# A two-layer mixing trunk on one core: rows by transposes of spread columns, weights cast ahead of the modulated input, two of u's weights split inside the first step

## The chip, the core and the metric

The kernel runs on one core of a Trainium2 chip. The core has five engines with a queue each: TensorE (PE, matmuls; PEld is its weight load), VectorE (DVE), ScalarE (ACT), GpSimd (POOL) and SyncE (SP), which here only issues DMAs. The metric is the device time of one execution in microseconds (us). The kernel before takes 1035.68 us, the median of three runs (1033.89 to 1036.2).

## What is computed

Two layers over x (512 tokens by 1024 features) and a conditioning row c of 1024:

```
mod = silu(c) @ ada_w[l] + ada_b[l]           # 6 rows of 1024: shift, scale, gate, twice
h   = x * (1 + scale1) + shift1
a, u, v = split(h @ w_in[l])                  # 512 features each
y_a = pool_mixer(a)                           # trailing means over 2, 4, 8, 16 tokens, a 128x128 product, a scale
y_b = gelu(u) * (tril(W_s) @ norm(gelu(v)) + b)
x   = layernorm(2**0.5 * x + gate1 * ([y_a, y_b] @ w_out[l]))
h   = x * (1 + scale2) + shift2
g, val = split(h @ w_up[l])                   # 2816 features each
x   = layernorm(2**0.5 * x + gate2 * ((gelu(conv3(g)) * val) @ w_down[l]))
```

## The kernel before

**Products in three parts.** Every large product of a weight w and an activation h is made of three matmuls on rounded float32 (float32r): w_hi h_hi, w_hi h_lo and w_lo h_hi. A weight arrives as a tile `raw` of 128x1024 (512 KB) by DMA. ACT casts it to `whi` (L158), DVE subtracts to get `wlo` (L161). `refill` does this for the next weight of a fixed list `order`; `get` hands the oldest split weight out. There are four `raw` tiles and six pairs `whi`, `wlo`; a weight split "in units" takes tiles of 128x512 from the pool of 29 `unit` tiles instead. The engines run their queues in the order in which the code is written; nothing is reordered by a scheduler.

**The modulation row by row sums.** `mod` is not made on PE. A tile of `ada_w` (128 outputs by 1024 inputs, 512 KB) is multiplied on DVE by the row `c2` (2 silu(c), the same on all partitions) and summed along the row (`ada_sum`, L208): one sum gives 128 values, as one column of `modc`. There are 96 sums. 16 of them (shift and scale of the first norm) belong to the first step below. The others are put between other work by `pump(n)`; 24 of those (gate 1, scale 2, shift 2 of layer 0) must be done before the first norm's result is modulated. The text calls them sum 1 to sum 24. Sums read from seven tiles: three `ada` and, until x is loaded into them, four `xr`. `ada_load` fills tiles that are free, and waits on SP for the sum that read the tile before.

**Rows on all partitions.** `c2` is made by 16 matmuls of spread columns of c (hi and lo) against an identity, into two banks, and two copies on ACT (L97 to L109). Eighteen matmuls `idle` follow. A gate must be a row on all partitions too: `gate_start` makes, on DVE, four 128x512 tiles of identity times columns (L229 to L235), and `ada_flush`, two calls later, sums them on PE by a product with ones (L256, L257), two copies on ACT (L258).

**The first step.** The a and v parts of layer 0's input projection run over the eight 128-feature slices k of h. For each k: two sums, the columns A0 and B0 (L500, L503), then on ACT h_hi (L504) and h in full (L505), then on DVE h_lo (L508). `FIRST[k]` lists the weights that come in at step k: 0 to 3 are a's, 8 to 11 are v's (4 to 7 are u's and come after). In a step the code writes: h of k+1, h_lo of k, the casts and subtractions of the weights for k+1, and then the matmuls of k.

**After it** come, in layer 0, the copies of a (L592), pooling on DVE (`pool_group`), the norm of v on ACT, the four tiles of u (`u_tile`, 24 matmuls each), the pool products (`pool_mix`, L615), the gating products (`z_mms`), then the out projection: its first half is `project` (L369 to L371, tile out), its second `project_and_norm` (tile n_pj), in which the first norm waits for the gate and for all 24 sums. `MIX_FILL` and `OUT_FILL` say how many sums are pumped at each place. The gated MLP follows, and layer 1.

Of the kernel before, what the change touches and what calls it, by code (L numbers as in the profile page):

```python
# [26 lines left out]
FIRST = ((8, 0), (1,), (9, 2), (3,), (10,), (), (11,), ())  # L27
N_UNITS, N_RAW, N_ADA, N_SPLIT = 29, 4, 3, 6
AHEAD, N_IDLE = 2, 18
X_AT = 14  # L30
MIX_FILL, OUT_FILL = (3, 3, 3, 2, 1, 1), (2, 3, 3, 3)
# [8 lines left out]
def trunk(ctx: ExitStack, tc: tile.TileContext, a: dict, out: bass.AP):  # L40
# [52 lines left out]
    c_hl = [const.tile([P, KD], F32R, name=f"c_{n}") for n in ("hi", "lo")]  # L93
    V.tensor_copy(c_hl[0], c_th)
    V.tensor_tensor(c_hl[1], c_th, c_hl[0].bitcast(F32), op=ALU.subtract)
    c2 = const.tile([P, D], F32, name="c2")
    for hf in range(2):  # L97
        ps = bank(f"c2_{hf}")
        for j in range(4):
            k = 4 * hf + j  # L100
            for i, part in enumerate(c_hl):
                T.matmul(
                    ps[:, j * P : (j + 1) * P],
                    part[:, k : k + 1].to_broadcast([P, P]),
                    ident_r,
                    start=i == 0,
                    stop=i == 1,
                )
        A.copy(c2[:, halves(hf)], ps)  # L109

    idle = bank("idle")
    for i in range(N_IDLE):
        T.matmul(idle[:, :P], ident_r, ident_r, start=True, stop=True)
    ones_r = const.tile([P, P], F32R, name="ones_r")
    V.tensor_copy(ones_r, ones)
# [8 lines left out]
    for l in range(L):  # L124
        w_in = (0, 1, 2, 3, 8, 9, 10, 11) if l else [i for f in FIRST for i in f]
        order += [("w_in", (l, i)) for i in (*w_in, 4, 5, 6, 7)]
        order += [("w_out", (l, hf, i)) for hf in range(2) for i in range(4)]
        for j0, j1 in STAGES:
            order += [("w_up", (l, j, gv)) for j in range(j0, j1) for gv in range(2)]
            order += [("w_down", (l, hf, i)) for hf in range(2) for i in range(j0 // 2, j1 // 2)]  # L130
# [93 lines left out]
    def gate_start(l, v):  # L224

        g = modc[l][:, 8 * v : 8 * v + 8]
        gh = small.tile([P, KD], F32R, tag="gh", name=f"gh{l}_{v}")
        gl = small.tile([P, KD], F32R, tag="gl", name=f"gl{l}_{v}")
        V.tensor_copy(gh, g)  # L229
        V.tensor_tensor(gl, g, gh.bitcast(F32), op=ALU.subtract)  # L230
        out_ = []
        for hf in range(2):
            for part in (gh, gl):
                d = unit(f"gd{l}_{v}_{hf}", F32R)
                V.tensor_tensor(  # L235
                    d.rearrange("p (j n) -> p j n", j=4),
                    ident.unsqueeze(1).to_broadcast([P, 4, P]),
                    part[:, 4 * hf : 4 * hf + 4].bitcast(F32).unsqueeze(2).to_broadcast([P, 4, P]),
                    op=ALU.mult,
                )  # L240
                out_.append(d)
        return out_

    def ada_flush(now=False):


        for due in ada_due:
            due[0] += 1
            if due[3] is None and (now or due[0] >= 2):
                due[3] = gate_start(*due[1:3])  # L250
        while ada_due and (now or ada_due[0][0] >= 4):
            _, l, v, d = ada_due.pop(0)
            gates[l, v] = rows.tile([P, D], F32, tag="gate", name=f"gate{l}_{v}")
            for hf in range(2):
                ps = bank(f"gate{l}_{v}_{hf}")
                T.matmul(ps, ones_r, d[2 * hf], start=True, stop=False)  # L256
                T.matmul(ps, ones_r, d[2 * hf + 1], start=False, stop=True)  # L257
                A.copy(gates[l, v][:, halves(hf)], ps)  # L258

    def pump(n=1, upto=None):  # L260

        for _ in range(n):
            i = ada_at["step"]
            if i >= len(ada) or (upto is not None and ada[i][:2] not in upto):
                return
            ada_load(len(ada_free))
            l, v, n_ = ada[i]
            ada_sum(l, v, n_, ada_raw.pop(0))
            if n_ == KD - 1:
                o = slice(8 * v, 8 * v + 8)  # L270
                V.tensor_tensor(modc[l][:, o], modc[l][:, o], cols[l][:, C_ADAB + 8 * v : C_ADAB + 8 * v + 8], op=ALU.add)
                if v in (2, 5):
                    ada_due.append([0, l, v, None])
            ada_at["step"] += 1
# [210 lines left out]
    def first_load(k):  # L485

        if k >= KD:
            ada_load(len(ada_free))
            return
# [78 lines left out]
    for l in range(L):  # L568
# [156 lines left out]
        else:  # L725
            refill(1)
# [175 lines left out]
```

## Time and profile before

| | us |
|---|---|
| median of three runs | 1035.68 |
| the profiled execution | 1035.5 |
| its span, first to last instruction | 1033.8 |
| PE busy in it | 992.7 (96%) |
| DVE busy | 661.8 (64%) |
| ACT busy | 363.5 (35%) |
| POOL busy | 104.1 (10%) |

The profiled execution is 1.7 us longer than its span, and 0.2 us under the median. Times within it are counted from the span's start. The first 200 us are the part in which PE is not always busy: PE is at 9 tenths or more in 35 of the page's 40 slices, and four of the five others lie before 200 us. A wait is put down to what ended it; a row of a timeline gives start, length, engine, line, operation, and in brackets the idle time before it with what ended that.

### The profile page before, as it was taken

Reading aid. Unit: us, or ns where it says so; the run is one execution under the profiler, and the core shown is the slowest. Engines: PE = TensorE matmul, PEld = TensorE weight load, DVE = VectorE, ACT = ScalarE, POOL = GpSimd, SP = SyncE. Lnnn points to the kernel's source line nnn. Section 1 sums busy time; section 2 is a strip of 40 time slices with the busy share of each in tenths; the row PEclk is TensorE's granted clock in tenths of the full one; section 3 lists DMA queues with packets and bytes.
Section 4 is the critical chain, followed back from the end, with each engine's and each line's share of the span. In section 5 each row is a group of like instructions: output and inputs, shape, how many; then the busy total and the mean of one; then the engine's idle time right before and its main releaser. Section 6 shows DMA issues by size and latency. Waiting matters only on the chain.

```text
span 1033.8 us, 11992 instructions
## 1 busy us (share of the span) xinstructions
PE 992.7 (96%) x4676; PEld 828.6 (80%) x4676; DVE 661.8 (64%) x931; ACT 363.5 (35%) x531; POOL 104.1 (10%) x80
## 2 busy tenths in 40 slices
PE   7999868999999999999999999999999999999996
PEld 5777657888888888888889878898888888888886
DVE  5769877887771466747589763978554245544456
ACT  4362317433431123334155440743343222333210
POOL 0020003600000000000038100360000000000002
PEclk9999979999999999999999999999999999999999
DMA  9876553375563335546413321326332333223302
GB/s 354 322 246 207 207 207 122 107 281 205 204 223 102 101 130 188 193 154 253 163 61 116 129 73 62 102 102 229 118 102 82 102 101 98 90 98 102 123 1 81
DMA packets 46232, 153.54 MB, mean 149 GB/s; under 512 B 7264, under 2 KB 7520, under 8 KB 46176
## 3 DMA queue, kind: packets, MB, share of 16 engines
q1 hardware_dynamic: 46176, 152.78, 42.3%
q8 instruction: 36, 0.59, 0.2%
q14 instruction: 20, 0.16, 0.1%
HBM read 150.67 MB, written 2.10 MB: 148 GB/s over the span
## 4 chain that ended last, share of the span: by engine, by line
PE 82%; DVE 10%; DMA 2%; ACT 2%; issue 2%; POOL 1%; SPq 0%; DVEq 0%; POOLq 0%
PE up L197 15%; PE up L198 15%; PE up L196 15%; PE down L370 6%; PE down L371 6%; PE down L369 6%; DVE wlo L161 2%; PE u L198 1%; DVE xr L208 1%; DMA ada<-in_ada_w_dram 1%; PE u L196 1%; PE u L197 1%; PE n_pj L371 1%; PE n_pj L370 1%; PE n_pj L369 1%
## 5 line engine op out<-in xcount | busy, mean ns | idle before, releaser
L197 PE MATMUL up<-hl,whi 128*128 128x512 f32 (+1 forms) x768 | 286.1, 372 | 2.3 <-DVE hl L346 2.3
L198 PE MATMUL up<-hh,wlo 128*128 128x512 f32 (+1 forms) x768 | 286.0, 372 | 1.4 <-DVE wlo L161 1.4
L196 PE MATMUL up<-hh,whi 128*128 128x512 f32 (+1 forms) x768 | 286.3, 373 | 0.0
L161 DVE TENSOR_TENSOR wlo<-raw_w_up,whi 128x1024 fp32r<-128x1024 f32 x88 | 118.6, 1353 | 138.2 <-ACT whi L158 138.2
L197 PEld LDWEIGHTS up<-hl,whi 128*128 128x128 f32 x768 | 145.4, 189 | 27.5 <-DVE hl L346 2.7
L198 PEld LDWEIGHTS up<-hh,wlo 128*128 128x128 f32 x768 | 145.4, 189 | 26.6 <-DVE wlo L161 1.8
L196 PEld LDWEIGHTS up<-hh,whi 128*128 128x128 f32 x768 | 145.5, 189 | 25.1
L161 DVE TENSOR_TENSOR wlo<-raw_w_down,whi 128x1024 fp32r<-128x1024 f32 x44 | 53.9, 1225 | 114.0 <-ACT whi L158 114.0
L158 ACT CAST whi<-raw_w_up 128x1024 fp32r<-128x1024 f32 x88 | 90.9, 1045 | 57.0 <-PE down L371 52.6
L369 PE MATMUL down<-whi,gh 128*128 128x512 f32 x272 | 105.8, 389 | 0.0
L370 PE MATMUL down<-wlo,gh 128*128 128x512 f32 x272 | 105.8, 389 | 0.0
L371 PE MATMUL down<-whi,gl 128*128 128x512 f32 x272 | 105.8, 389 | 0.0
L208 DVE SCALAR_TENSOR_TENSOR ada<-ada,c 128x1024 f32<-128x1024 f32 x80 | 97.0, 1217 | 8.6 <-DMA ada<-in_ada_w_dram 4.5
L796 ACT ACTIVATE y<-y 128x512 f32<-128x512 f32 x44 | 27.9, 633 | 152.0 <-DVE y L793 152.0
L158 ACT CAST whi<-raw_w_down 128x1024 fp32r<-128x1024 f32 x44 | 46.0, 1047 | 74.3 <-PE down L371 74.3
L786 ACT ACTIVATE y<-up,cols 128x512 f32<-128x512 f32 x44 | 34.3, 779 | 80.5 <-PE up L198 80.5
L343 ACT ACTIVATE ht_n<-tr_n,B,A 128x128 f32<-128x128 f32 x96 | 36.0, 455 | 67.3 <-PE tr_n L331 67.3
L369 PEld LDWEIGHTS down<-whi,gh 128*128 128x128 f32 x272 | 51.1, 188 | 10.7
L370 PEld LDWEIGHTS down<-wlo,gh 128*128 128x128 f32 x272 | 51.1, 188 | 10.6
L371 PEld LDWEIGHTS down<-whi,gl 128*128 128x128 f32 x272 | 51.1, 188 | 10.5
L304 POOL TENSOR_SCALAR rs_n<-mv_n 128x1 f32<-128x1 f32 x12 | 7.2, 601 | 497.6 <-DVE mv_n L302 497.6
L161 DVE TENSOR_TENSOR wlo<-raw_w_in,whi 128x1024 fp32r<-128x1024 f32 x24 | 37.6, 1587 | 22.3 <-ACT whi L158 22.3
(169 smaller groups left out, 1469.4 us busy)
## 6 DMA issues: line engine op xcount, KB each, us to landing
raw_w_up<-in_w_up_dram SPq DMA_DIRECT2D x88, 512.0 KB, 3.7
ada<-in_ada_w_dram SPq DMA_DIRECT2D x80, 512.0 KB, 3.8
raw_w_down<-in_w_down_dram SPq DMA_DIRECT2D x44, 512.0 KB, 3.7
raw_w_in<-in_w_in_dram SPq DMA_DIRECT2D x24, 512.0 KB, 5.8
xr<-in_ada_w_dram SPq DMA_DIRECT2D x16, 512.0 KB, 7.0
raw_w_out<-in_w_out_dram SPq DMA_DIRECT2D x16, 512.0 KB, 4.5
xT<-in_xT_dram SPq DMA_DIRECT2D x8, 256.0 KB, 8.9
xr<-in_x_dram SPq DMA_DIRECT2D x4, 512.0 KB, 4.9
```

The costliest lines, as they stand in the source:

```text
L158: A.copy(hi, src)
L161: (eng or V).tensor_tensor(lo, src, hi.bitcast(F32), op=ALU.subtract)
L196: T.matmul(ps, w[0], x[0], start=start, stop=False)
L197: T.matmul(ps, w[0], x[1], start=False, stop=False)
L198: T.matmul(ps, w[1], x[0], start=False, stop=stop)
L208: V.scalar_tensor_tensor(raw, raw, 0.5, c2, op0=ALU.mult, op1=ALU.mult, accum_out=modc[l][:, o : o + 1])
L343: A.activation(tmp[:, w], ps[hf][:, w], AF.Identity, bias=cb[:, k : k + 1], scale=ca[:, k : k + 1])
L369: T.matmul(ps[:, f], ah[:, cs], wh, start=i + j == 0, stop=False)
L370: T.matmul(ps[:, f], ah[:, cs], wl, start=False, stop=False)
L371: T.matmul(ps[:, f], al[:, cs], wh, start=False, stop=i + j == n - 1)
L786: A.activation(y, pg, AF.Identity, bias=col[:, C_CB + j : C_CB + j + 1], scale=col[:, cw + 2 : cw + 3])
L796: A.activation(y, y, AF.Gelu_apprx_tanh)
```

## The change

- `c2` and the gates are made by one function, `spread`: a column of 128 values, read as if it stood 128 times side by side, is transposed on PE against the float32 identity, which gives the row on all partitions; eight transposes and two copies for 1024 values. The hi and lo columns of c, `gate_start`, its tiles and `ones_r` go. Five idle matmuls stand before c2's transposes and twenty behind them; c2's second half is copied by DVE.
- In the first step the casts of the weights for k+1 are written ahead of h of k+1, and their subtractions behind A0 and B0 and ahead of h_lo of k+1. h_lo of k+1 is written in step k, before k's matmuls.
- Weights 4 and 5 (u's first two) come in at steps 5 and 7 of the first step, split in units.
- A gate is transposed at the second `ada_flush` after its last sum, not the fourth.
- `pump` loads one tile fewer than are free. In the last two steps of the first step `first_load` loads two and three tiles.
- `MIX_FILL` is (6, 3, 2, 2, 1, 1) for (3, 3, 3, 2, 1, 1), `OUT_FILL` (2, 2, 3, 2) for (2, 3, 3, 3).

```diff
-FIRST = ((8, 0), (1,), (9, 2), (3,), (10,), (), (11,), ())
+FIRST = ((8, 0), (1,), (9, 2), (3,), (10,), (4,), (11,), (5,))
-AHEAD, N_IDLE = 2, 18
+AHEAD, N_IDLE = 2, (5, 20)
-MIX_FILL, OUT_FILL = (3, 3, 3, 2, 1, 1), (2, 3, 3, 3)
+MIX_FILL, OUT_FILL = (6, 3, 2, 2, 1, 1), (2, 2, 3, 2)
...
+    def spread(to, col, second=A.copy):
+        for hf in range(2):
+            ps = bank("spread")
+            for j in range(4):
+                k = 4 * hf + j
+                T.transpose(ps[:, j * P : (j + 1) * P], col[:, k : k + 1].to_broadcast([P, P]), ident)
+            (second if hf else A.copy)(to[:, halves(hf)], ps)
...
+    idle_mms(N_IDLE[0])
+    spread(c2, c_th, V.tensor_copy)
+    idle_mms(N_IDLE[1])
...
     def ada_flush(now=False):
         for due in ada_due:
             due[0] += 1
-            if due[3] is None and (now or due[0] >= 2):
-                due[3] = gate_start(*due[1:3])
-        while ada_due and (now or ada_due[0][0] >= 4):
-            _, l, v, d = ada_due.pop(0)
+        while ada_due and (now or ada_due[0][0] >= 2):
+            _, l, v = ada_due.pop(0)
             gates[l, v] = rows.tile([P, D], F32, tag="gate", name=f"gate{l}_{v}")
-            for hf in range(2):
-                ps = bank(f"gate{l}_{v}_{hf}")
-                T.matmul(ps, ones_r, d[2 * hf], start=True, stop=False)
-                T.matmul(ps, ones_r, d[2 * hf + 1], start=False, stop=True)
-                A.copy(gates[l, v][:, halves(hf)], ps)
+            spread(gates[l, v], modc[l][:, 8 * v : 8 * v + 8])
...
-            ada_load(len(ada_free))
+            ada_load(len(ada_free) - 1)
...
         if k >= KD:
-            ada_load(len(ada_free))
+            ada_load(k - KD + 2)
             return
...
+    def first_w(k, defer=None):
+        for i in FIRST[k]:
+            refill(1, None, defer, in_units=3 < i < 8)
...
-    refill(len(FIRST[0]), None, late)
+    refill(1, None, late)
     first_h(0, *firsts[0])
-    for f in late:
-        f()
+    late.pop()()
+    refill(1, None, late)
+    first_lo(0)
+    late.pop()()
...
         if k + 1 < KD:
+            first_w(k + 1, late)
             first_h(k + 1, *firsts[k + 1])
-        first_lo(k)
-        refill(len(FIRST[k + 1]) if k + 1 < KD else 1)
+            for f in late:
+                f()
+            late.clear()
+            first_lo(k + 1)
...
+    ready[:0] = u_w
...
         else:
-            refill(1)
             pump(MIX_FILL[0], fill)
```

**ACT, the first step's beginning.** Before (whi are casts of weights, hh is h_hi, the write to xT is h in full; whi_177, 180 and 207 are weights 8, 0 and 1):

```order
L158 CAST whi_177<-raw_w_in_167 128x1024
L158 CAST whi_180<-raw_w_in_169 128x1024
L504 ACTIVATE hh<-xT_165,B_0_158,A_0_157 128x512
L505 ACTIVATE xT_165<-xT_165,B_0_158,A_0_157 128x512
L504 ACTIVATE hh<-xT_173,B_0_158,A_0_157 128x512
L505 ACTIVATE xT_173<-xT_173,B_0_158,A_0_157 128x512
L158 CAST whi_207<-raw_w_in_175 128x1024
```

Now (whi_170, 180, 194 are the same weights):

```order
L156 CAST whi_170<-raw_w_in_160 128x1024
L475 ACTIVATE hh<-xT_158,B_0_151,A_0_150 128x512
L476 ACTIVATE xT_158<-xT_158,B_0_151,A_0_150 128x512
L156 CAST whi_180<-raw_w_in_162 128x1024
L156 CAST whi_194<-raw_w_in_168 128x1024
L475 ACTIVATE hh<-xT_166,B_0_151,A_0_150 128x512
L476 ACTIVATE xT_166<-xT_166,B_0_151,A_0_150 128x512
```

The cast of weight 0 has gone behind h of k = 0, and the cast of weight 1 ahead of h of k = 1.

**DVE, from the last h_lo of the first step to the pooling** (ada and xr with modc are the sums, wlo the weights' low parts, ws the pooling). Before:

```order
L508 TENSOR_TENSOR hl<-xT_365,hh 128x512
L508 TENSOR_TENSOR hl<-xT_402,hh 128x512
L161 TENSOR_TENSOR wlo_481<-raw_w_in_478,whi_480 128x1024
L611 TENSOR_SCALAR psc_532<-cols_87 128x1 x4
L161 TENSOR_TENSOR wlo_540<-raw_w_in_508,whi_539 128x1024
L208 SCALAR_TENSOR_TENSOR ada_80,modc_153<-ada_80,c_106 128x1024
L208 SCALAR_TENSOR_TENSOR xr_81,modc_153<-xr_81,c_106 128x1024
L208 SCALAR_TENSOR_TENSOR xr_82,modc_153<-xr_82,c_106 128x1024
L602 TENSOR_TENSOR ws_0_550<-at_524 128x511
```

Now:

```order
L479 TENSOR_TENSOR hl<-xT_406,hh 128x512
L593 TENSOR_SCALAR psc_537<-cols_87 128x1 x4
L206 SCALAR_TENSOR_TENSOR ada_80,modc_146<-ada_80,c_102 128x1024
L206 SCALAR_TENSOR_TENSOR xr_81,modc_146<-xr_81,c_102 128x1024
L206 SCALAR_TENSOR_TENSOR xr_82,modc_146<-xr_82,c_102 128x1024
L206 SCALAR_TENSOR_TENSOR xr_83,modc_146<-xr_83,c_102 128x1024
L206 SCALAR_TENSOR_TENSOR xr_84,modc_146<-xr_84,c_102 128x1024
L206 SCALAR_TENSOR_TENSOR ada_78,modc_146<-ada_78,c_102 128x1024
L584 TENSOR_TENSOR ws_0_556<-at_529 128x511
```

The low parts of weights 4 and 5 (wlo_481, wlo_540) have gone from here into the first step, and three more sums stand ahead of the pooling.

**DVE, in the out projection, from the last low part of mix (ml) on.** Before:

```order
L667 TENSOR_TENSOR ml_856<-z_852,mh_855 128x512
L161 TENSOR_TENSOR wlo_896<-raw_w_out_840,whi_895 128x1024
L208 SCALAR_TENSOR_TENSOR ada_79,modc_153<-ada_79,c_106 128x1024
L208 SCALAR_TENSOR_TENSOR ada_80,modc_153<-ada_80,c_106 128x1024
L229 CAST gh_2_929<-modc_153 128x8
L230 TENSOR_TENSOR gl_2_930<-modc_153,gh_2_929 128x8
L235 TENSOR_TENSOR gd_2_0_933<-ident,gh_2_929 128x512
L235 TENSOR_TENSOR gd_2_0_935<-ident,gl_2_930 128x512
L235 TENSOR_TENSOR gd_2_1_937<-ident,gh_2_929 128x512
L235 TENSOR_TENSOR gd_2_1_939<-ident,gl_2_930 128x512
L161 TENSOR_TENSOR wlo_942<-raw_w_out_862,whi_941 128x1024
L208 SCALAR_TENSOR_TENSOR ada_78,modc_153<-ada_78,c_106 128x1024
```

Now:

```order
L649 TENSOR_TENSOR ml_872<-z_868,mh_871 128x512
L159 TENSOR_TENSOR wlo_913<-raw_w_out_856,whi_912 128x1024
L206 SCALAR_TENSOR_TENSOR ada_78,modc_146<-ada_78,c_102 128x1024
L242 TENSOR_TENSOR modc_146<-modc_146,cols_87 128x8
L206 SCALAR_TENSOR_TENSOR ada_79,modc_146<-ada_79,c_102 128x1024
L159 TENSOR_TENSOR wlo_948<-raw_w_out_878,whi_947 128x1024
L206 SCALAR_TENSOR_TENSOR ada_80,modc_146<-ada_80,c_102 128x1024
L206 SCALAR_TENSOR_TENSOR ada_78,modc_146<-ada_78,c_102 128x1024
```

The six instructions of the gate are gone; the sums that follow are numbers 16 on, where before they were 14 on. (The row with modc and cols adds the bias.)

## Rows read from the trace of the kernel before

**Rows 1.** Busy us: PE, PEld, DVE, ACT, POOL (instructions); granted clock, DMA share, GB/s

```profile
62.45:122.67 60.22, 55.68 (x240) 43.20 (x239) 53.84 (x98) 25.73 (x46) 6.71 (x9) 0.97 0.60 202
...
122.67:147.76 25.09, 14.02 (x49) 10.20 (x47) 19.34 (x36) 1.64 (x2) 0.79 (x2) 0.80 0.74 271
...
200.00:1033.80 833.80, 820.92 (x3861) 688.13 (x3859) 510.32 (x677) 281.92 (x399) 68.59 (x49) 1.00 0.38 131
```

**Rows 2.** Waits of PE from 0 to 200 us: total, times, longest

```profile
PE n_pj L370 <- DVE wlo L161: 7.5, 2, 5.1
```

**Rows 3.** Timeline, PE, the first turn: start, length, engine, line, operation [idle <- releaser]

```profile
147.76 1.09 PE L331 MATMUL tr_n<-ident,xr 128*128 128x128 f32 x8 [3.59 <-DVE xr L416]
```

**Rows 4.** Timeline, DVE and ACT, one k of the first step

```profile
33.39 1.22 DVE L208 SCALAR_TENSOR_TENSOR ada<-ada,c 128x1024 f32<-128x1024 f32 x1
...
35.87 0.68 DVE L508 TENSOR_TENSOR hl<-xT,hh 128x512 fp32r<-128x512 f32 x1
...
35.99 0.82 ACT L504 ACTIVATE hh<-xT,B,A 128x512 fp32r<-128x512 f32 x1 [3.78 <-DVE B L503]
...
38.63 1.23 DVE L161 TENSOR_TENSOR wlo<-raw_w_in,whi 128x1024 fp32r<-128x1024 f32 x1 [2.08 <-ACT whi L158]
...
39.77 1.22 DVE L208 SCALAR_TENSOR_TENSOR xr<-xr,c 128x1024 f32<-128x1024 f32 x1
```

**Rows 5.** Timeline, ACT and PE, where the first step begins

```profile
9.62 1.04 ACT L158 CAST whi<-raw_w_in 128x1024 fp32r<-128x1024 f32 x1 [2.18 <-DMA raw_w_in<-in_w_in_dram]
...
10.89 1.04 ACT L158 CAST whi<-raw_w_in 128x1024 fp32r<-128x1024 f32 x1 [0.23 <-DMA raw_w_in<-in_w_in_dram]
...
13.30 0.75 PE L546 MATMUL a<-hh,wlo 128*128 128x512 f32 x1
...
16.90 1.09 PE L549 MATMUL v<-whi,hl 128*128 128x512 f32 x4
```

**Rows 6.** Busy us by stretch, 10 to 20 us

```profile
10.00:20.00 10.00, 7.05 (x23) 4.87 (x23) 7.23 (x12) 5.80 (x7) 0.00 (x0) 1.00 1.03 411
```

**Rows 7.** Timeline, PE, the first products of u's tiles and the pool products

```profile
62.45 0.39 PE L196 MATMUL u<-hh,whi 128*128 128x512 f32 x1
...
67.89 1.02 PE L645 MATMUL rw<-wst,ones 128*128 128x512 f32 x2
...
74.20 0.39 PE L196 MATMUL u<-hh,whi 128*128 128x512 f32 x1
...
84.08 1.88 PE L615 MATMUL pm<-ws,poolw 128*128 128x512 f32 x4
...
91.29 1.02 PE L615 MATMUL pm<-ws,poolw 128*128 128x512 f32 x2
```

**Rows 8.** Timeline, ACT and DVE, between the first step and u's third tile

```profile
61.06 2.06 ACT L592 COPY at<-a 128x512 f32<-128x512 f32 x4 [1.12 <-PE a L549]
...
68.67 0.69 DVE L602 TENSOR_TENSOR ws<-at 128x511 f32<-128x511 f32 x1
...
72.50 1.04 ACT L158 CAST whi<-raw_w_in 128x1024 fp32r<-128x1024 f32 x1
...
76.08 1.22 DVE L161 TENSOR_TENSOR wlo<-raw_w_in,whi 128x1024 fp32r<-128x1024 f32 x1
```

**Rows 9.** Timeline, SP, issues of the small constants

```profile
53.45 0.67 SPq L578 DMA_DIRECT2D poolw<-in_pool_w_dram  x1
...
62.79 0.58 SPq L66 DMA_DIRECT2D raw_w_in<-in_w_in_dram  x1
```

**Rows 10.** Loads into the tiles ada, 0 to 145 us

```profile
DMA to landing us min/median/max: 3.2/5.2/9.6
```

**Rows 11.** Timeline, DVE, end of the out projection to the first norm

```profile
116.08 1.22 DVE L161 TENSOR_TENSOR wlo<-raw_w_out,whi 128x1024 fp32r<-128x1024 f32 x1
...
123.32 1.22 DVE L208 SCALAR_TENSOR_TENSOR ada<-ada,c 128x1024 f32<-128x1024 f32 x1
...
141.72 0.68 DVE L321 TENSOR_TENSOR res<-out,gate 128x512 f32<-128x512 f32 x1
```

More of the change, by code (lines that the diff above doesn't have):

```diff
@@ L92, in trunk, with idle_mms @@
     V.scalar_tensor_tensor(c_th, c_th, 1.0, c_in, op0=ALU.add, op1=ALU.mult)
-    c_hl = [const.tile([P, KD], F32R, name=f"c_{n}") for n in ("hi", "lo")]
-    V.tensor_copy(c_hl[0], c_th)
-    V.tensor_tensor(c_hl[1], c_th, c_hl[0].bitcast(F32), op=ALU.subtract)
     c2 = const.tile([P, D], F32, name="c2")
-    for hf in range(2):
[L98 to L109, printed above, removed]
-    idle = bank("idle")
[L112 to L115, printed above, removed]
+    def spread(to, col, second=A.copy):
[5 more added lines that the diff above has]
+            (second if hf else A.copy)(to[:, halves(hf)], ps)
+    idle = bank("idle")
+    def idle_mms(n):
+        for i in range(n):
+            T.matmul(idle[:, :P], ident_r, ident_r, start=True, stop=True)
+    idle_mms(N_IDLE[0])
+    spread(c2, c_th, V.tensor_copy)
+    idle_mms(N_IDLE[1])
     neg_half = const.tile([P, 1], F32, name="neg_half")
@@ L125, in trunk @@
         w_in = (0, 1, 2, 3, 8, 9, 10, 11) if l else [i for f in FIRST for i in f]
-        order += [("w_in", (l, i)) for i in (*w_in, 4, 5, 6, 7)]
+        order += [("w_in", (l, i)) for i in (*w_in, *(i for i in range(4, 8) if i not in w_in))]
         order += [("w_out", (l, hf, i)) for hf in range(2) for i in range(4)]
@@ L222, in ada_load @@
                 ada_at["load"] += 1
[L224 to L242, printed above, removed]
     def ada_flush(now=False):
@@ L272, in pump @@
                 if v in (2, 5):
-                    ada_due.append([0, l, v, None])
+                    ada_due.append([0, l, v])
             ada_at["step"] += 1
@@ L508, in first_lo @@
         V.tensor_tensor(hl[:, k, :], firsts[k][0], hh[:, k, :].bitcast(F32), op=ALU.subtract)
+    def first_w(k, defer=None):
+        for i in FIRST[k]:
+            refill(1, None, defer, in_units=3 < i < 8)
     v_ps = [bank(f"v0_{c}") for c in range(NCH)]
-    a_ps, a_w, v_w, firsts, late = [], [], [], [], []
+    a_ps, a_w, v_w, u_w, firsts, late = [], [], [], [], [], []
     for k in range(2):
         first_load(k)
-    refill(len(FIRST[0]), None, late)
+    refill(1, None, late)
     first_h(0, *firsts[0])
-    for f in late:
-        f()
+    late.pop()()
+    refill(1, None, late)
+    first_lo(0)
+    late.pop()()
     for k in range(KD):
@@ L521, in trunk @@
         for i in FIRST[k]:
-            w = get()
-            if i < 8:
+            if i >= 8:
+                v_w.append(get())
+            elif i < 4:
                 a_ps.append(bank(f"a0_{i}"))
-                a_w.append(w)
+                a_w.append(get())
             else:
-                v_w.append(w)
+                u_w.append(get())
         if k + 1 < KD:
+            first_w(k + 1, late)
             first_h(k + 1, *firsts[k + 1])
-        first_lo(k)
-        refill(len(FIRST[k + 1]) if k + 1 < KD else 1)
+            for f in late:
+                f()
+            late.clear()
+            first_lo(k + 1)
         for ps, w in zip(a_ps[old:], a_w[old:]):
```

1 line of the change is left out of this document (removed).

## The prediction

> **What bounds the kernel now.** I read the busy time by stretch first, then PE's waits, then the timelines of DVE, ACT and PE where PE waits.
>
> From 200 us on PE is busy 820.92 of 833.80 us at a granted clock of 1.00, and DVE 510 [rows 1]. Work that is taken from DVE or ACT there frees nobody. Before it, from 62.45 to 147.76 us, DVE is busy 73.2 of 85.3 us, and from 122.67 on PE works only 14.02 of 25.09 us, at a mean granted clock of 0.80, between its levels of 1.2 and 2.4 GHz [rows 1]. PE's largest wait there is for low parts of weights, 7.5 us [rows 2], which stand on DVE behind sums. The first norm's result is turned at 147.76, after a wait of 3.59 us for DVE [rows 3]. So DVE's order sets the end of the first norm, and what follows hangs on that. I cut the way to 147.76 into four stretches, and the sum is the shift of that row.
>
> **First step, up to u (62.45 us).** In one k DVE does two sums and the columns (33.39 to 35.87, 2.48 us), h_lo (0.68), then waits 2.08 us for a cast that ACT does only after h, and makes one low part (38.63 to 39.77, 1.14): a period of 6.38 us [rows 4]. With the cast ahead of h, the low part starts at once. h takes ACT two passes of about 0.82 [rows 4], so h_lo is free some 1.75 us after the columns, 0.6 after the low part. The period becomes 2.48 + 1.14 + 0.6 + 0.65 = 4.9 us.
>
> The beginning pays for it. Weight 8 is cast at 9.62, when it lands; weight 0 lands at 10.89 [rows 5]. Now h of k = 0 comes between them: 10.66 to about 12.35 on ACT, then weight 0 until 13.4, its low part until 14.65. PE's second product needs that; before, it ran at 13.30 [rows 5]. From there to the end of k = 0 (16.90 and four products of 0.227, 17.81) it is 4.5 us, part of it at half pace [rows 5]: end at 19.15. Weight 1 lands 1.83 MB after weight 0; at 411 GB/s [rows 6] that is 4.5 us, 15.4, so its cast ends at 16.4, and k = 1 finds all it needs. 24 products take 67.89 - 62.45 = 5.44 us [rows 7], 0.2267 each. k = 1 to 7 have 21, 27, 33 and four times 24, 177 in all, 40.1 us: u begins at 59.3 instead of 62.45, if nothing is late. The one close place is the low part of weight 2, ready about 24.35 by the chain above, wanted at 24.4. From k = 3 on DVE is ahead: h of k = 7 is ready at about 18 + 6 x 4.9 + 1.1 = 48.5, wanted at 53.9. That slack of 5 us also covers weights 4 and 5, whose casts now ride in ACT's and DVE's free time.
>
> Gain 3.15 us. Bounds: +3.8 if the first products lose nothing to the new order; -1.7 if PE stays at half pace through k = 1 as well (21 x 0.23 = 4.8 us more). I take 3.15, since rows 5 shows the pace to come back within the first 15 products.
>
> c2 by eight transposes instead of sixteen matmuls I cost at nothing either way: h of k = 0 waits for ACT's cast at 9.62 [rows 5]. If that cover went, the price would be the sums' own time, two of 1.2 us [rows 4].
>
> **u and the pool products, to 91.29 us.** Before, u's first tile takes 5.44, ones times W_s and the second tile 6.31 (67.89 to 74.20), the third 9.88 (to 84.08), the first two pool products and the fourth tile 7.21 [rows 7]. The third is 4.44 over 5.44: it waits for the low part at 76.08, which stands behind five DVE pieces that began at 68.67 (two poolings and three sums, 7.41 us) [rows 8], and then runs at half pace for a while. Now three more sums stand ahead of the poolings, six in all. Five have their tiles loaded within the first step, and run from about 50 us, when DVE has nothing else; the load of the sixth is issued behind u's other weights and the small constants, a block of 9.3 us before [rows 9], which can begin when weight 5 lands (15.4 + 5.7 + 5 x 4.5 = 43.5); 5.2 us for its landing [rows 10] make 58. So poolings and three sums end at 59.2 + 7.4 = 66.6. The cast for that third tile came 11.44 us after the copies of a [rows 8], with the cast of weight 5 (1.04) in it. It starts at 57.9 + 10.4 = 68.3; low part by 70.6. The tile starts at 59.3 + 5.44 + 6.31 = 71.05 and wants the low part 0.45 later. The wait goes, by a margin of 0.9 us.
>
> Added on PE: gate 1's transposes behind the third tile, eight, 1.09 us as the eight at 147.76 [rows 3]. So the second pair of pool products comes at 59.3 + 5.44 + 6.31 + 5.44 + 1.09 + 7.21 = 84.8, instead of 91.29: gain 6.5 us so far.
>
> **Mixing to the out projection, 91.29 to 116.08.** From the pool products each step waits for the one before (PE, ACT's high part, cast, DVE's low part, gating, cast), with as many sums between as before. I carry its 24.79 us [rows 7, 11] over: 109.6.
>
> **The last sums, 116.08 to 147.76.** Before, 116.08 to 123.32 (7.24 us) holds a low part, sums 14 and 15, the gate's pieces and another low part [rows 11]. Sums 14 and 15 are now in the mixing, where DVE waits for casts anyway; the gate's pieces are gone; the second low part moves in among the later sums. 1.14 us is left, so sum 16 starts at 110.7, 12.6 us earlier. From there to the first norm's residual it is 18.40 us before [rows 11]. Nine sums, two low parts and the columns are 9 x 1.2 + 2 x 1.14 + 0.6 = 13.7 us; the other 4.7 are waits for loads, since only three tiles are left for the sums (the `xr` tiles hold x by then). A tile is filled when its sum is done, and the load takes 5.2 us in the median [rows 10]. The third low part (1.14) falls into these waits, so I keep 18.40, then 6.04 to the turn [rows 3, 11]: 135.1 instead of 147.76. PE is not later than that: the second block of products starts after the last low part, and there were 3.59 us to spare.
>
> Here the Trainium skill has another price. Its page DMA: Bandwidth & Descriptors (Anatomy of one DMA) puts a transfer at about 2.0 us fixed and bytes over 436 GB/s; for 512 KB that makes 3.2 us, an estimate by that page. The 26 loads here took 3.2 at least and 5.2 in the median [rows 10], so the trace agrees only with its best case. By the page the waits would vanish, which is the first rival below.
>
> **The rest.** Three more gates are made after 200 us: four matmuls become eight transposes, at most 0.2 us of PE each [rows 3]; DVE's pieces were hidden. `pump` now leaves one tile empty, which puts each load behind the next weight on SP; with a sum every few us after 200 that is hidden too. Eight more `unit` tiles are held until u's second tile is done; from 71 us on they are free. I cost all of this at nothing, bounds +-0.6.
>
> **Sum.** 147.76 - 135.1 = 12.6 us. The profiled execution took 1035.5 us, 1.7 beyond its span: 1022.9. It lies 0.2 under the median of the runs, so I say 1023.
>
> **Rivals.**
> 1. The last sums find their tiles loaded. The shallower queue of loads (half of 411 GB/s is unused before 122 us [rows 1, 6]) may land them nearer the 3.2 of rows 10. Then sum 16 to the residual is work alone, with the third low part 14.8 instead of 18.4: 3.6 us more gain, 1019.3. Against it: the same weights share the queue in that stretch, at 271 GB/s on the mean [rows 1].
> 2. The loads come a step later. A tile left empty costs up to one sum, 1.2 us, in each of the two rounds of three tiles: 2.4 us, 1025.4. For it: PE waits there for what stands on DVE behind such sums [rows 2].
> 3. The sixth sum blocks DVE. If the block of small constants starts no earlier than before, at 53.45 [rows 9], the load lands at 68, the low part of u's third tile comes at 77.8 instead of being wanted at 71.5, and 6.3 us are lost: 1029.3. It decides from a landing at 61 us on. Against it: the five loads ahead of that block wait for sums that are done by 43 us.
> 4. Slower than before: the cast ahead of h turns on ACT. Its queue is served in order, so h of k + 1 waits until the weight for k + 1 has landed and, from weight 10 on, until PE has let go of a pair of split tiles. If that ring (weight tile, cast, h, sums, next load) makes the period of k longer than 8.4 us, h of k = 7 comes at 69.5 and more, u starts 12.6 us later than in my chain, and all is lost: 1036 and up. The period before was 6.38 [rows 4], and the loads need 4.5 a k at 411 GB/s; that speaks against it.
>
> **Chances.** Forecast 0.58, rival 1 0.13, rival 2 0.14, rival 3 0.10, rival 4 0.05. A measurement of this kernel tells 0.2% (2.1 us) from no change. Rival 4 gives 0.03 slower and, at periods little under its point, 0.02 within 0.2%; rivals 1 to 3 and the forecast are faster: 0.95. For 8 times in 10 the range takes rivals 1 and 2 with 1.5 us beside them for the open pace at the start, and leaves out rivals 3 and 4: 1018 to 1028.5.
>
> **What would show it.** In the profile of the changed kernel: low parts in the first step without a wait for their cast, and a period near 4.9 us; u's first product near 59.3; no PE wait for a low part in u's third tile; the gate's instructions gone from DVE; sum 16 near 110.7 and the first turn near 135.1; after 200 us no change of PE. Wrong would be: h waiting on ACT behind a cast that waits for a load; a sum before the poolings waiting for its load beyond 61 us; or the turn moved by less than the starts of u and of the pool products say.

## The result, and the profile after

The changed kernel takes 1023.95 us in the median of 4 runs (1023.64 to 1025.23), the kernel before 1035.78 beside it: a ratio of 0.9892, 95% interval 0.9875 to 0.9909, so 11.8 us faster. The forecast was 1023. The profiled execution spans 1021.9 us in place of 1033.8.

Busy time by stretch of the changed kernel; the stretches answer to those of [rows 1], each begins and ends at the same piece of work or near it (columns: PE, PEld, DVE, ACT, POOL with instructions; granted clock, DMA share, GB/s):

```profile
59.40:109.50 50.10, 48.33 (x223) 38.43 (x222) 42.52 (x79) 25.29 (x46) 4.97 (x8) 1.00 0.61 223
109.50:136.27 26.77, 17.77 (x70) 13.57 (x69) 21.13 (x38) 1.06 (x1) 0.79 (x2) 0.94 0.71 254
```

The first is 10 us shorter than the 60.22 of before; the second, with the last sums, is no shorter than the 25.09 there. The gain lies ahead of 109.5 us. Timeline of PE after, u's first product, the second pool products and the first turn (start, length, [idle <- releaser]), against [rows 3, 7]:

```profile
59.40 0.39 PE L194 MATMUL u<-hh,whi 128*128 128x512 f32 x1
...
84.72 1.88 PE L597 MATMUL pm<-ws,poolw 128*128 128x512 f32 x4
...
136.27 0.30 PE L302 MATMUL tr_n<-ident,xr 128*128 128x128 f32 x1 [3.62 <-DVE xr L387]
```

62.45 became 59.40, 91.29 became 84.72, 147.76 became 136.27: gains of 3.05, 6.57 and 11.49 us. PE still waits 3.6 us for DVE at the turn, as in [rows 3]. DVE and ACT in one k of the first step, against [rows 4]:

```profile
28.41 0.69 DVE L479 TENSOR_TENSOR hl<-xT,hh 128x512 fp32r<-128x512 f32 x1 [0.59 <-ACT xT L476]
...
30.93 1.05 ACT L156 CAST whi<-raw_w_in 128x1024 fp32r<-128x1024 f32 x1 [2.55 <-DMA raw_w_in<-in_w_in_dram]
...
32.02 1.23 DVE L159 TENSOR_TENSOR wlo<-raw_w_in,whi 128x1024 fp32r<-128x1024 f32 x1 [0.43 <-ACT whi L156]
...
33.58 0.69 DVE L479 TENSOR_TENSOR hl<-xT,hh 128x512 fp32r<-128x512 f32 x1 [0.34 <-ACT xT L476]
```

The wait of 2.08 us for a cast is down to 0.43, here with a load that ACT itself waits for; this period is 5.2 us, and the next h_lo, at 38.49 and 43.40, are 4.9 us apart. From its second product (13.97 us) to 107.29 us PE waits for nothing. DVE after, from the end of the first step:

```profile
49.16 1.22 DVE L206 SCALAR_TENSOR_TENSOR ada<-ada,c 128x1024 f32<-128x1024 f32 x1
...
59.11 1.22 DVE L206 SCALAR_TENSOR_TENSOR ada<-ada,c 128x1024 f32<-128x1024 f32 x1 [4.13 <-DMA ada<-in_ada_w_dram]
...
69.58 1.23 DVE L159 TENSOR_TENSOR wlo<-raw_w_in,whi 128x1024 fp32r<-128x1024 f32 x1 [1.63 <-ACT whi L156]
```

Five sums run from 49.16, the sixth waits for its load until 59.11, and the low part of u's third tile stands at 69.58 in place of 76.08 [rows 8]; PE no longer waits for it. The tail of the sums, from sum 16 to the first norm's residual, against [rows 11]:

```profile
109.50 1.22 DVE L159 TENSOR_TENSOR wlo<-raw_w_out,whi 128x1024 fp32r<-128x1024 f32 x1
110.64 1.22 DVE L206 SCALAR_TENSOR_TENSOR ada<-ada,c 128x1024 f32<-128x1024 f32 x1
...
113.13 1.22 DVE L159 TENSOR_TENSOR wlo<-raw_w_out,whi 128x1024 fp32r<-128x1024 f32 x1
...
117.44 1.22 DVE L159 TENSOR_TENSOR wlo<-raw_w_out,whi 128x1024 fp32r<-128x1024 f32 x1
...
123.07 1.22 DVE L159 TENSOR_TENSOR wlo<-raw_w_out,whi 128x1024 fp32r<-128x1024 f32 x1
125.69 1.22 DVE L206 SCALAR_TENSOR_TENSOR ada<-ada,c 128x1024 f32<-128x1024 f32 x1 [1.39 <-DMA ada<-in_ada_w_dram]
...
128.22 1.23 DVE L206 SCALAR_TENSOR_TENSOR ada<-ada,c 128x1024 f32<-128x1024 f32 x1 [1.30 <-DMA ada<-in_ada_w_dram]
...
130.13 0.68 DVE L292 TENSOR_TENSOR res<-out,gate 128x512 f32<-128x512 f32 x1
```

From sum 16 (110.64) to the residual (130.13) it is 19.49 us, 1.1 more than before. Three low parts stand among the sums here, two before.

### The profile page after: what moved, and what is told of

The parts are those of the page before. It is cut to its first block, busy times and chain, and to the rows that moved or that the text cites. A ratio compares the mean times of both kernels' runs of the same rounds, so it can differ in the third digit from the quotient of the medians.

```text
span 1021.9 us, 12000 instructions
## 1 busy us (share of the span) xinstructions
PE 986.9 (97%) x4691; PEld 826.8 (81%) x4691; DVE 650.2 (64%) x907; ACT 364.0 (36%) x532; POOL 102.6 (10%) x80
## 4 chain that ended last, share of the span: by engine, by line
PE 85%; DVE 9%; DMA 2%; ACT 1%; issue 1%; POOL 1%; SPq 0%; DVEq 0%; POOLq 0%; ACTq 0%
PE up L195 15%; PE up L196 15%; PE up L194 15%; PE down L342 6%; PE down L341 6%; PE down L340 6%; PE v L527 2%; PE u L196 1%; PE u L195 1%; PE u L194 1%; DVE wlo L159 1%; DVE res L292 1%; PE a L527 1%; DVE stn L381 1%; DMA ada<-in_ada_w_dram 1%
## 5 line engine op out<-in xcount | busy, mean ns | idle before, releaser
L781 ACT CAST gh<-y 128x512 fp32r<-128x512 f32 x44 | 27.3, 621 | 43.7 <-DVE y L779 43.7
```

## The experiments

Each kernel's time stands against runs of the kernel before on the same chip; the other columns are rows of its profiled execution, in us: the starts of u's first product, of the second pair of pool products, of sum 16 and of the first turn (the transposes of the first norm's result). "Tail" is sum 16 to the residual. The profiled execution need not be a middle one: it was the slowest of its kernel's in old_gates (1026.82), late_x (1029.35) and best (1020.91), the fastest in h_first (1026.78), four (1021.49) and start (1021.24).

| kernel | median | ratio, 95% interval | u | 2nd pool pair | sum 16 | tail | first turn |
|---|---|---|---|---|---|---|---|
| before | 1035.78 | | 62.45 | 91.29 | 123.32 | 18.40 | 147.76 |
| changed | 1023.95 | 0.9892, 0.9875–0.9909 | 59.40 | 84.72 | 110.64 | 19.49 | 136.27 |
| h_first | 1027.71 | 0.9924, 0.9912–0.9936 | 63.37 | 88.95 | 114.88 | 18.65 | 139.66 |
| fills | 1026.29 | 0.9907, 0.9894–0.9920 | 59.06 | 83.50 | 112.95 | 18.94 | 138.02 |
| deep | 1024.38 | 0.9887, 0.9873–0.9902 | 59.63 | 84.94 | 110.86 | 20.10 | 137.09 |
| four | 1023.28 | 0.9877, 0.9863–0.9890 | 59.33 | 84.64 | 110.62 | 17.12 | 134.40 |
| no_u | 1032.62 | 0.9964, 0.9950–0.9977 | 59.92 | 94.21 | 120.13 | 18.94 | 145.21 |
| old_gates | 1024.01 | 0.9890, 0.9874–0.9906 | 60.69 | 85.13 | 112.70 | 19.51 | 138.26 |
| start | 1022.26 | 0.9867, 0.9854–0.9879 | 58.73 | 84.05 | 109.97 | 18.01 | 134.12 |
| late_x | 1027.93 | 0.9923, 0.9909–0.9936 | 60.33 | 85.65 | 111.57 | 20.27 | 137.99 |
| before_swap | 1033.33 | 0.9973, 0.9962–0.9984 | 62.00 | 86.96 | 119.74 | 18.33 | 144.11 |
| no_u2 | 1023.05 | 0.9877, 0.9863–0.9891 | 58.94 | 84.54 | 110.46 | 18.63 | 135.23 |
| cap | 1020.42 | 0.9853, 0.9839–0.9867 | 59.29 | 84.61 | 110.53 | 17.16 | 133.83 |
| best | 1019.48 | 0.9842, 0.9828–0.9856 | 59.19 | 84.50 | 110.47 | 15.92 | 132.53 |

First, parts undone, and the tail.

**h_first**

```diff
-            first_w(k + 1, late)
             first_h(k + 1, *firsts[k + 1])
-            for f in late:
-                f()
-            late.clear()
             first_lo(k + 1)
+            first_w(k + 1)
```

> The changed kernel with one part undone: from k = 1 on, h is made ahead of the casts of that step's weights again (the beginning, the moved sums, the split of weights 4 and 5 inside the step stay). Theory (the cast's place gives the start of u, and DVE's chain carries it to the first turn): the period of k goes back from 4.9 to about 6.4 us, u's first product from 59.4 to 62 or 63, and the first turn from 136.3 to about 139.5; 1027 us. Rival (PE's own work sets the start of u, the period had slack): u at most 1.5 us later, first turn before 138; 1024 to 1025.5 us.

One period of DVE in h_first:

```profile
33.15 1.23 DVE L159 TENSOR_TENSOR wlo<-raw_w_in,whi 128x1024 fp32r<-128x1024 f32 x1 [0.25 <-ACT whi L156]
...
38.60 0.69 DVE L479 TENSOR_TENSOR hl<-xT,hh 128x512 fp32r<-128x512 f32 x1 [1.74 <-ACT xT L476]
39.54 1.23 DVE L159 TENSOR_TENSOR wlo<-raw_w_in,whi 128x1024 fp32r<-128x1024 f32 x1 [0.25 <-ACT whi L156]
```

The period is 6.39 us again. u comes 3.97 us later and the first turn 3.39: the theory, with a start of u a little over its range. The idle time that is back in a period stands ahead of h_lo (1.74 us) and only 0.25 us of it ahead of the low part: h_lo of k + 1 is still written in step k, where the kernel before wrote it a step later and waited 2.08 us for the cast [rows 4].

**fills**

```diff
-MIX_FILL, OUT_FILL = (6, 3, 2, 2, 1, 1), (2, 2, 3, 2)
+MIX_FILL, OUT_FILL = (3, 3, 3, 2, 1, 1), (2, 3, 3, 3)
```

> The changed kernel with the old table of sums: three ahead of the poolings in place of six, thirteen up to the out projection in place of fifteen, eleven in the out projection in place of nine. Theory (DVE's order sets the first turn): u's third tile still has no wait, since u starts early and the poolings only come sooner; two sums more after the mixing cost two sums of 1.2 us and at most as much again in waits for their loads: first turn 138.7 to 141, 1026.3 to 1028.5 us. Rival (the six sums ahead of the poolings were what took away the wait of the third tile): a wait for a low part in the third tile is back, pool products 3 us later, 1027 us and over with the loss already at the second pair of pool products (after 87, in place of 84.7).

No wait in u's third tile, sum 16 2.31 us later and the turn 1.75: two sums moved past the mixing cost two sums, and the turn, at 138.02, is a little under the theory's range. The six ahead of the poolings did not take away the wait.

**deep**

```diff
-            ada_load(len(ada_free) - 1)
+            ada_load(len(ada_free))
```

> The changed kernel, but each sum fills every free tile before it runs (no tile left empty). Theory A (the tile left empty makes the loads of the last sums late; that is why sum 16 to the residual took 19.5 us in place of 18.4): the stretch shrinks to 18.4 or less, first turn near 135.1, 1022.8 us. Theory B (the queue that the loads share with weights makes them late): loads go one sum earlier but land as late, and weights behind them on the queue land later; within 0.5 us of the changed kernel, 1023.5 to 1025 us.

The tail is not shorter but 20.10, 0.6 more. Theory A falls: the tile left empty does not make the loads late. That deeper loading costs time is not shown: the turn is 0.8 us later, more than theory B said, but the intervals of the times overlap almost wholly.

**four**

```diff
-N_UNITS, N_RAW, N_ADA, N_SPLIT = 29, 4, 3, 6
+N_UNITS, N_RAW, N_ADA, N_SPLIT = 27, 4, 4, 6
```

> The changed kernel with four tiles for the sums in place of three, and 27 shared unit tiles in place of 29 (for the room). Theory A (too few tiles: a load can start only when a sum lets go of its tile, which makes 4.4 us of waits in the last nine sums): the waits go to under 1.5 us, the residual comes 3 us earlier, first turn near 133, 1020.5 to 1021.5 us. Theory B (the shared queue is the limit there): the loads start earlier but take longer, the waits stay over 3.5 us, 1023 to 1025 us. If two fewer unit tiles stall an engine in the mixing, the loss is seen before 109.6 us, where sums after the mixing begin.

DVE's waits for loads in the tail fell from 4.4 to 2.1 us, between the two theories, and the turn came 1.9 us earlier, but the interval of the times overlaps that of the changed kernel, and kernels with the same loads in the tail scatter between 18.0 and 19.5 us. Alone it settles nothing.

Next: u's weights, the gate, the beginning, and x.

**no_u** (weights 4 and 5 not split in the first step)

```diff
-FIRST = ((8, 0), (1,), (9, 2), (3,), (10,), (4,), (11,), (5,))
+FIRST = ((8, 0), (1,), (9, 2), (3,), (10,), (), (11,), ())
...
             first_lo(k + 1)
+        else:
+            refill(1)
...
+            refill(1)
             pump(MIX_FILL[0], fill)
```

> The changed kernel with weights 4 and 5 left out of the first step: they are cast and halved as in the kernel before, the last cast of the step in its last k, the next at the start of u. Theory (the wait of u's third tile went because its cast no longer has that of weight 5 before it, beside u's earlier start): the low part of the third tile comes at least one cast and one low part (1.04 and 1.14 us) later, a wait of 1 to 4 us stands in u's third tile again, and the second pair of pool products, sum 16 and the first turn all come that much later: 86 to 89, 112 to 115, 137 to 140; 1025 to 1028 us. Rival (six sums ahead of the poolings are what matters, the split is hidden work only moved): no wait in u over 0.5 us, 1023.5 to 1024.5 us.

The wait came back with 6.1 us, and the turn fell 8.9 us behind, more than twice the 0.7 to 3.7 that were expected. DVE and then ACT of no_u show why:

```profile
52.13 0.33 DVE L595 TENSOR_SCALAR psc<-cols 128x1 f32<-128x1 f32 x4
61.56 1.23 DVE L159 TENSOR_TENSOR wlo<-raw_w_in,whi 128x1024 fp32r<-128x1024 f32 x1 [9.10 <-ACT whi L156]
62.70 1.22 DVE L206 SCALAR_TENSOR_TENSOR ada<-ada,c 128x1024 f32<-128x1024 f32 x1
```

```profile
58.53 2.06 ACT L576 COPY at<-a 128x512 f32<-128x512 f32 x4 [7.57 <-PE a L532]
60.45 1.08 ACT L156 CAST whi<-raw_w_in 128x1024 fp32r<-128x1024 f32 x1
```

The low part of u's second weight stands ahead of six sums in DVE's queue. Its cast stands behind the copies of a, which wait for PE's last product of the step. So DVE does nothing for 9.10 us, and the sums, whose tiles are loaded (no_u2, below, runs them from 52.14 without a wait), start at 62.70. The kernel before had the same hole, in two pieces (DVE, before):

```profile
59.97 1.23 DVE L161 TENSOR_TENSOR wlo<-raw_w_in,whi 128x1024 fp32r<-128x1024 f32 x1 [5.73 <-ACT whi L158]
...
64.09 1.22 DVE L161 TENSOR_TENSOR wlo<-raw_w_in,whi 128x1024 fp32r<-128x1024 f32 x1 [2.65 <-ACT whi L158]
65.23 1.22 DVE L208 SCALAR_TENSOR_TENSOR ada<-ada,c 128x1024 f32<-128x1024 f32 x1
```

That is 8.38 us of idle DVE, with three sums behind it. The Trainium skill, Perfetto Trace Analysis (Tensor Engine Instruction), says in a note that the queues of ACT, DVE and GpSimd are served strictly in order; the 9.10 us agree.

**old_gates** (the gates' two functions as before)

```diff
...
-            spread(gates[l, v], modc[l][:, 8 * v : 8 * v + 8])
+            for hf in range(2):
+                ps = bank(f"gate{l}_{v}_{hf}")
+                T.matmul(ps, ones_r, d[2 * hf], start=True, stop=False)
+                T.matmul(ps, ones_r, d[2 * hf + 1], start=False, stop=True)
+                A.copy(gates[l, v][:, halves(hf)], ps)
...
```

> The changed kernel with the gates made as before (high and low part, four products with the unit matrix on DVE, four matmuls with ones), c2 still by transposes. Theory (DVE's order sets the first turn, so the pieces of the gate, about 2.7 us on DVE, stand on the way): gate 1's pieces come ahead of the last pooling or in the mixing; sum 16 and the first turn 1.5 to 2.7 us later, 1025.3 to 1026.7 us. Rival (DVE's waits for casts in the mixing hide the pieces): within 0.5 us of the changed kernel at the first turn, 1023.5 to 1024.5 us.

Sum 16 and the turn are 2 us later, but u was already 1.29 later, ahead of any gate: ACT's first cast got its load 0.60 us later (9.72 for 9.12), and k = 0 took the rest longer. Counted from u, sum 16 comes 0.77 us later and the turn 0.70, between theory and rival, and the times show no difference.

**start** (both weights of k = 0 cast ahead of its h)

```diff
-    refill(1, None, late)
+    refill(2, None, late)
     first_h(0, *firsts[0])
-    late.pop()()
-    refill(1, None, late)
+    for f in late:
+        f()
+    late.clear()
     first_lo(0)
-    late.pop()()
```

> The changed kernel with both weights of k = 0 cast ahead of its h, as before; from k = 1 on casts stay ahead of h. Theory (the new order at k = 0 costs PE what its second product comes later, 13.97 for 13.30): the second product at 13.3, u's first product 0.3 to 0.8 us earlier than 59.4, all else moved by the same; 1023.2 to 1023.7 us. Rival (h of k = 0 now comes later, behind the cast of weight 0, and PE's third and later products wait for its low part instead): u's first product at 59.4 or later, 1024 us and over.

PE in start:

```profile
12.14 0.79 PE L527 MATMUL a<-hh,whi 128*128 128x512 f32 x1 [2.87 <-ACT hh L475]
12.74 0.75 PE L527 MATMUL a<-hh,wlo 128*128 128x512 f32 x1
```

The second product runs at 12.74 in place of 13.97, and u 0.67 us earlier, as the theory said. For u one trace is not enough: its start lies between 58.94 and 60.69 in the eight kernels with the changed kernel's beginning, between 58.73 and 59.29 in the three with this one (start, cap, best). The turn gains 2.15, the rest of it in a shorter tail (18.01), which puts the time, 1022.26, under the theory's range. The interval of its times overlaps that of the changed kernel a little.

**late_x**

```diff
-X_AT = 14
+X_AT = 20
```

> The changed kernel with one number changed: the four tiles that get x in the end serve the sums one turn longer (x is loaded in them when 20 loads of the sums' weights are issued, not 14). The third of a fourth tile gave 1.9 us at the first turn with the queue full from 110 to 128, and a deeper queue alone lost 0.8. Theory A (what makes the last nine sums wait is that x is fetched from 86 to 108, where the queue has room, and the sums' weights from 110 on, where it has none; x is wanted only from the residual on): waits of the last sums under 1.5 us in place of 4.4, residual near 127, first turn 133 to 134, 1020.5 to 1021.8 us. Theory B (whatever is loaded there, the queue is full: x takes the place of the sums' weights): the residual waits for x instead, first turn within 0.7 us of 136.3, 1023.3 to 1024.7 us. Theory C (x, queued in order, holds up weights of the out projection behind sums that are not done): PE waits more for low parts of these weights, later than the changed kernel, over 1025 us.

Slower, and by no theory as written. SP and DVE in late_x:

```profile
112.82 1.67 SPq L213 DMA_DIRECT2D xr<-in_x_dram  x2
114.59 0.38 SPq L66 DMA_DIRECT2D raw_w_out<-in_w_out_dram  x1
116.45 1.47 SPq L213 DMA_DIRECT2D xr<-in_x_dram  x2
118.01 0.38 SPq L66 DMA_DIRECT2D raw_w_up<-in_w_up_dram  x1
118.45 1.75 SPq L76 DMA_DIRECT2D ada<-in_ada_w_dram  x2
```

```profile
126.09 1.22 DVE L206 SCALAR_TENSOR_TENSOR ada<-ada,c 128x1024 f32<-128x1024 f32 x1 [5.09 <-DMA ada<-in_ada_w_dram]
```

Sums 16 to 21 indeed run without a wait, but x's loads are queued ahead of the last sums' weights, and sum 22 waits 5.09 us for its load. It is C's order with another victim. The profiled execution loses some 2.4 us more at a turn at 660 us (a wait of 4.8 us, 2.5 in the changed kernel); the cause of that is open.

Last: the place of the low part, and the queue in the tail.

**before_swap** (in the kernel before)

```diff
-            refill(1)
             pump(MIX_FILL[0], fill)
+            refill(1)
             pool_group(0)
```

> The kernel before, with two lines exchanged: the three sums ahead of the poolings are given out before the cast and low part of u's second tile, not behind them. Theory (the low part stands in DVE's queue ahead of the sums and waits there for its cast, which ACT does only behind the copies of a; DVE idles 2.65 us for it, and all that follows is late): the sums run in that idle time, the poolings begin 2.6 us earlier, the wait of u's third tile goes; second pair of pool products 87 to 88.5 in place of 91.29, first turn 143.5 to 145, 1031 to 1033 us. Rival (what removed the wait was the weights' split inside the first step, not the place of a low part among sums): the wait stays, pool products within 1 us of 91.29, 1034.5 us and over.

The wait in u goes from 2.5 to 0.2 us, the second pool products come at 86.96, the turn at 144.11. The time gains 1.7 to 3.9 us by its interval; the median, 1033.33, is just over the theory's range, and the profiled execution, 1031.29, is one of the faster of the ten. From u to the second pool products the two lines save 3.88 us (28.84 to 24.96); the whole change, with gate 1's transposes in it, saves 3.52.

**no_u2** (no_u, with the same lines exchanged)

```diff
-            refill(1)
             pump(MIX_FILL[0], fill)
+            refill(1)
```

> The kernel of the earlier experiment without the split of weights 4 and 5 in the first step (first turn 145.2, 1032.6 us), with the same two lines exchanged: the six sums ahead of the cast and low part of u's second tile. Theory (the 9 us that experiment lost are the 9.1 us for which DVE idled behind that low part, with the six sums behind it): DVE does the sums from about 52 us on, the low part follows at 62 to 63, in time for u's second tile; no wait over 0.5 us in u's second and third tile, second pair of pool products 85 to 86.5, first turn 136.5 to 138.5, 1024 to 1026 us. Rival (the casts have to be off ACT and DVE there, as the low parts of u's tiles are the bound, wherever they stand): a wait of 2 us and more stays in u, first turn over 140.

DVE in no_u2:

```profile
52.14 1.22 DVE L206 SCALAR_TENSOR_TENSOR ada<-ada,c 128x1024 f32<-128x1024 f32 x1
...
58.30 1.22 DVE L206 SCALAR_TENSOR_TENSOR ada<-ada,c 128x1024 f32<-128x1024 f32 x1
...
60.58 1.22 DVE L159 TENSOR_TENSOR wlo<-raw_w_in,whi 128x1024 fp32r<-128x1024 f32 x1 [1.06 <-ACT whi L156]
```

The six sums fill the hole, the low part waits 1.06 us, and nothing in u is late: 1023.05 for 1032.62, and a turn at 135.23, both a little better than the theory said. No gain of the split of weights 4 and 5 inside the first step by itself shows (1023.95 with it, the intervals overlap); it is one of two ways to get a waiting low part out from ahead of the sums.

**cap** (start, and no loads for the up projection before the sums are given out)

```diff
-    raws, ready = [], []
+    raws, ready, cap = [], [], [20]
...
-                while count["load"] < min(len(order), count["split"] + count["ahead"]):
+                while count["load"] < min(cap[0], count["split"] + count["ahead"]):
...
         pump(len(ada), fill)
+        cap[0] = len(order)
```

> The kernel with both weights of k = 0 cast ahead of its h (1022.3 us, sum 16 to the residual 18.0 us), and no weights of the up projection loaded until the last sums are given out: two loads of 512 KB less on the queue between 110 and 128 us. Theory (the queue is full there, so each load that is not needed makes the last sums wait): 1.3 to 2.6 us less from sum 16 to the residual (15.5 to 16.8), first turn about 132 to 133, 1020 to 1021 us. Rival (a sum waits for its own load's time from issue to landing, with three tiles, not for the queue): 17.5 to 19.5 us as the other kernels, 1022 to 1023 us; or the up projection's first weights come late and PE waits for their casts after 135 us, 1023 us and over.

**best** (cap, with the edit of four)

> The same, with four tiles for the sums in place of three besides (27 shared unit tiles). Theory: the nine sums find nearly all loads landed, sum 16 to the residual is work alone, 14.8 to 16 us, and PE's second half of the out projection is next to bound, since its low parts stand among these sums: first turn 130.5 to 132, 1018.5 to 1020.5 us. Rival (load times on the full queue, not tiles or bytes): 17 us and over, 1021.5 to 1023 us.

cap stands on start, so start is what it is read against. Waits of DVE for the sums' loads from 110 to 140 us in the changed kernel, start, cap and best (total, times, longest):

```profile
DVE ada L206 <- DMA ada<-in_ada_w_dram: 4.4, 4, 1.4
```

```profile
DVE ada L206 <- DMA ada<-in_ada_w_dram: 3.0, 3, 2.0
```

```profile
DVE ada L206 <- DMA ada<-in_ada_w_dram: 2.1, 4, 0.8
```

```profile
DVE ada L206 <- DMA ada<-in_ada_w_dram: 0.9, 1, 0.9
```

Busy time from 110.6 to 126 us, start, cap and best:

```profile
110.60:126.00 15.40, 9.13 (x37) 6.87 (x36) 12.45 (x20) 1.05 (x1) 0.00 (x0) 0.94 0.90 312
```

```profile
110.60:126.00 15.40, 10.16 (x40) 7.68 (x40) 13.23 (x22) 1.05 (x1) 0.00 (x0) 0.94 0.81 273
```

```profile
110.60:126.00 15.40, 10.69 (x43) 8.11 (x42) 14.35 (x24) 2.10 (x2) 0.00 (x0) 0.94 0.92 349
```

With two loads fewer the DMA share falls from start's 0.90 to 0.81 and the waits from 3.0 to 2.1 us; a tail of 17.16 is 0.85 under start's, less than the 1.3 expected, and the intervals of the two times overlap. With a fourth tile it is 15.92 us, as expected, with waits of 0.9 us, though the queue is fuller there than in start (0.92, 349 GB/s): a full queue alone does not make the sums wait. The turn, at 132.53, is half a microsecond later than expected, and cap's, at 133.83, nearly one. best has the lowest median here: 16.3 us under before and 4.5 under the changed kernel, whose interval it leaves clear; cap's interval overlaps its own.

## Why the prediction was right

**The first step.** The chain held: k = 0 ends at 19.26 (said 19.15), k = 1 to 7 take 40.14 us (40.1), u starts at 59.40 (59.3). Undoing the order costs 3.97 us (h_first); the prediction has 3.8 for it, without the price of the new beginning. The good end of k = 0 is in part luck, two misses that cancel. The second product came at 13.97 for 14.65, 0.50 of it because ACT's first cast got its load at 9.12 in place of 9.62; from there to the end it took 5.29 us for 4.5, with products 0.43 us apart up to 17.98 and 0.23 apart after that (the half pace of the prediction; the profile gives a granted clock of 1.00 for both stretches). Counted from ACT's first cast, the second product comes 4.85 us later in the changed kernel and 3.70 in start, so the new beginning costs it 1.15 us; what of that is left at u, no run settles. c2 was free: ACT's first cast waits 4.46 us for its load after it; no run undoes c2's transposes.

**u's third tile.** The forecast row was right (84.8; 84.72), its reason incomplete. I let five sums "run from about 50 us, when DVE has nothing else" without saying what made that possible. It was not the earlier u, nor six sums for three: DVE had nothing else before either, for 8.38 us, behind low parts that waited for casts. no_u, no_u2 and before_swap show that this order alone makes the wait of the third tile and takes it away. DVE's timeline between 54 and 64 us shows it; the rows of DVE that the prediction reads [rows 8] begin at 68.67.

**The mixing.** 24.78 us from the second pool products to the low part at 109.50; 24.79 was carried over.

**The last sums.** Sum 16 at 110.64, said 110.7. fills gives two sums as 2.31 us. The gate's pieces, out of the tail's head, would cost only some 0.7 us where they would stand now (old_gates).

The term that was mis-sized is the tail: I kept 18.40, it measured 19.49, and with it the first turn came 1.1 us later than said. The step that failed is that the third low part "falls into these waits". Waits of DVE in the kernel before, from 122 to 142 us:

```profile
DVE ada L208 <- DMA ada<-in_ada_w_dram: 4.5, 4, 1.5
```

The changed kernel has 4.4: the waits stayed, and the low part's 1.14 us came on top. How much of it they hide is scatter. Without its waits the tail is 13.9 us in the kernel before, and 15.0 to 15.3 in the six kernels that have three low parts and the same loads there; their waits run from 3.0 us (start, a tail of 18.01) over 3.4 and 3.5 (no_u2, h_first) and 3.8 (no_u) to 4.3 and 4.4 (old_gates, 19.51, and the changed kernel).

Rival 2 (the tile left empty) is excluded by deep, rival 1 (tiles found loaded) by 4.4 us of waits. What shortens the waits is a fourth tile (four) or two loads fewer (cap), to 2.1 us each, and both together, to 0.9 (best). The Trainium skill's estimate by DMA: Bandwidth & Descriptors (Anatomy of one DMA), 3.2 us for 512 KB, is a fit for DMAs that GpSimd issues. These are issued by SP, and in the changed kernel not one load into `ada` up to 145 us was as quick:

```profile
DMA to landing us min/median/max: 3.5/5.9/9.6
```

**The other rivals.** Rival 3 needed the sixth sum later than 61 us; it ran at 59.11, 1.9 us from its point. Rival 4 needed a period over 8.4 us; it was 4.9, though casts do wait for loads (2.55 us above). Of the signs of being wrong, h behind a cast that waits for a load did occur, at 21.65 and 31.89 us, and cost h some 0.3 us each time; PE did not wait for it.

**The rest.** Of 11.49 us at the first turn, 11.77 are there at the last (159.76 for 171.53) and 11.9 in the span.

## What to carry to other kernels

Before asking what an engine has to do, look where it idles in a stretch it bounds, and what stands behind the instruction it waits for: a piece that waits for another engine belongs behind the independent work, not ahead of it. When a change does several things, a part may owe its gain to an order that it brings about by the way; undo it both with and without that order. Where sums wait for loads, a tile more and taking out loads that nobody needs yet shortened the waits here; filling the tiles one sum earlier did not.

## What the runs showed of the hardware

Much the same wait ahead of the first turn left PE at different levels of its clock. Granted clock of the 6.4 us from the turn on, changed kernel (after a wait of 3.62 us) and the kernel before (after 3.59 us):

```profile
136.27:142.67 6.40, 6.40 (x32) 5.37 (x33) 5.53 (x10) 4.16 (x10) 1.11 (x2) 1.00 0.00 0
```

```profile
147.76:154.16 6.40, 6.40 (x25) 5.28 (x26) 5.53 (x10) 4.15 (x10) 1.11 (x2) 0.73 0.00 0
```

1.00 is the level of 2.4 GHz, 0.73 a mean between 1.2 and 2.4 GHz. no_u had 0.73 too, after a wait of only 1.91 us, and old_gates 1.00 after 1.71 us. Full pace there put the next turn 1.6 us further ahead; PE gave most of it back, part of it in a wait of 1.67 us for a low part at 152.30 (0.70 us in the kernel before, at 164.07). What decides the level, no run here shows.
